# Two heads' small matmuls in turns on different rows or columns of TensorE's array, and one attention chain for two

## The chip, the cores and the metric

The kernel runs on one core of one Trainium2 chip. The metric is the device time of one execution in microseconds (us). The engines are TensorE (PE in the profile, its weight loads PEld), VectorE (DVE), ScalarE (ACT), GpSimd (POOL) and SyncE (SP). Each engine runs its own instructions in the order in which they stand in its queue; engines wait for each other by semaphores.

## The reference

Three layers on 256 tokens of width 1024, in float32. The first block is run twice: a mixer (gated delta rule and a dilated attention of 8 heads of 64) and a convolutional GLU. The second block has a mixer of three parts (gated linear attention of 4 heads with 32 key and 64 value channels, a causal convolution of width 31, a differential attention of 4 heads with two 64-wide maps each) and then a mixture of 16 experts. What the change touches, cut to its core:

```python
# first block, attention of 8 heads (three dilations, merged by their softmax denominators)
s = einsum('bqhd,bkhd->bhqk', q, k);  o = softmax(s + window) @ v
# second block, differential attention: two maps a head
a = softmax(q1 @ k1.T) - lam * softmax(q2 @ k2.T);  o = a @ v
# second block, gated linear attention, chunked in the reference
S_t = diag(alpha_t) S_{t-1} + k_t v_t^T;  o_t = q_t S_t
# which is  o = (q k^T, entry i,j times the product of alpha over j+1..i) v
```

## The kernel before

The work is one program on one core. Weights are streamed from memory, each split into a high and a low part (`wh` on ScalarE, L382, and `wl` on VectorE or GpSimd, L383), and every large product is three matmuls, L404 to L406. These fill the time between small dependent steps. In each layer a `Weave` object (L198) takes several generators ("chains") and one generator of filling matmuls: a chain yields a pair, the TensorE time that it has just used and the delay before it may go on; where no chain may go on, the filler does. Afterwards a scheduler orders each engine's instructions, so that the order on an engine is not that of the text.

The PSUM memory has eight banks, `bank(0)` to `bank(7)`, each 128 partitions of 512 floats; a bank is reused when its reader is done.

In the first mixer the chains are two of the delta rule, a preparation, two attention chains `attn(0)` and `attn(1)`, and the closing of the delta rule, `delta_out`, whose gated norm is `od` (L955). Each attention chain takes one head of a pair, `probs` (L574) computes two score matmuls (L575, 128 x 128; L576, 128 x 256) on rows 0 to 63 or 64 to 127 of the array, and the masked maxima; then the softmax goes over ScalarE and VectorE (`sm`, L1005 to L1010), three transposes (L326) put it into `pT`, and `mix_values` (L597 to L600) multiplies with the values, on columns 0 to 63 or 64 to 127. Chain 0 writes its half of bank 2, chain 1 the other half and then splits the result for the output projection. Bank 6 belongs to chain 0, bank 7 to chain 1.

In the second mixer two chains `diff(0)` and `diff(1)` do the same for the differential attention, two maps a head. The chain `gla` builds the linear attention's 4 score matrices level by level. The keys' and queries' factors of eight levels (`gX`, made on GpSimd, L1321 and L1322) give for each head and each pair of levels a block of matmuls of 32 rows (L1353; L1358 and L1361 for the last two levels; 16 blocks, twelve of L1353), in bank 3 for heads 0 and 2, in bank 4 for heads 1 and 3. After each block VectorE copies the blocks' valid parts to `gsc` under a mask (L1366). Ahead of the levels stand the diagonal blocks (L1335, L1336). The convolution's 62 taps (L1247) run on VectorE at the same time.

A matmul of 32-bit floats (without the high and low split) appears as two records in the trace.

Of the kernel before, what the change touches and what calls it, by code (L numbers as in the profile page):

```python
# [17 lines left out]
P = 128  # L18
S = 256
NT = 2  # L20
# [177 lines left out]
class Weave:  # L198
    """Lays several dependent chains and one stream of filling work into one trace order."""
# [48 lines left out]
def emit(ctx, tc, A, out, stop=None, dbg=None):  # L248
# [89 lines left out]
    def rsqrt1(ss, scale, o=None):  # L338
        """1 / sqrt(sum * scale + EPS) of one value a partition, whose sum comes in two parts."""
# [78 lines left out]
    def rows_in(t, xT, a, g, gain, done):  # L418
        """The residual step of token tile t, and its new rows, transposed and split."""
# [23 lines left out]
    def row_scales(nv, done, lag):  # L443
        """What the next norm scales the rows by: per row, and the same spread over the partitions."""
# [35 lines left out]
    def residual(t, a, g):  # L480
        """x += rmsnorm(a) * g on token tile t."""
# [31 lines left out]
    def tok_first(ps, chunks, xT, done, end, mid=None, ahead=None):  # L513
        """Two groups of products of token rows; those of the first rows go ahead of the second rows' norm."""
# [124 lines left out]
    def mixer1(l, before, held, a0):  # L639
# [355 lines left out]
        def attn(lane):  # L995
            yield lambda: "qkT" in done
            yield (0, 1.0 + 1.5 * lane)
            qT, kT = env["qk"][:, 0], env["qk"][:, 1]
            for pair in range(4):
                pr = slice(64 * lane, 64 * lane + 64)  # L1000
                hs = slice((2 * pair + lane) * 64, (2 * pair + lane) * 64 + 64)
                sm, nmx = probs(bank(6 + lane), qT[pr, pair, :], kT[pr, pair, :], cst[:, C_DB:C_DB + 384])
                ls = tmp([P, 2], tag="lsum")
                for t, (c0, c1) in enumerate(QT):
                    SC.activation(sm[:, c0:c1], sm[:, c0:c1], AF.Exp, bias=nmx[:, t:t + 1], scale=0.125)  # L1005
                    V.tensor_tensor_reduce(sm[:, c0:c1], sm[:, c0:c1], cst[:, C_DC + c0:C_DC + c1], 1.0, 0.0,
                                           op0=OP.mult, op1=OP.add, accum_out=ls[:, t:t + 1])
                V.reciprocal(ls, ls)
                for t, (c0, c1) in enumerate(QT):
                    V.tensor_scalar(sm[:, c0:c1], sm[:, c0:c1], ls[:, t:t + 1], None, op0=OP.mult)  # L1010
                yield (0.65, 3.2)
                pT = transpose_probs(6 + lane, sm)
                yield (0.33, 0.6)
                yield lambda: "v" in done
                if lane == 0:
                    env["po", pair] = bank(2)
                else:
                    yield lambda pair=pair: ("po", pair) in done
                po = env["po", pair]
# [912 lines left out]
```

## Time and profile before

| | us |
|---|---|
| median of 3 runs | 1104.01 (1103.96 to 1109.92) |
| span of the profiled execution | 1100.8 |
| median less that span | 3.2 |
| TensorE busy in it | 1052.8 (96%) |
| VectorE busy | 904.2 (82%) |
| ScalarE busy | 634.5 (58%) |
| GpSimd busy | 209.9 (19%) |

The profiled execution's own time is its span, from the first to the last instruction; the time of a run also has what lies around it, here 3.2 us by the median. The mean granted TensorE clock over the span is 0.960 of full speed, 2.4 GHz; the lower level is 1.2 GHz, a granted clock of 0.50.

In the profile the busy times say how full an engine is. The chain that ended last follows the end of the program back from step to step to what released it, so it says on which engine the time was spent. Windows give busy times stretch by stretch.

### The profile page before, as it was taken

Reading aid. Unit: us, or ns where it says so; the run is one execution under the profiler, and the core shown is the slowest. Engines: PE = TensorE matmul, PEld = TensorE weight load, DVE = VectorE, ACT = ScalarE, POOL = GpSimd, SP = SyncE. Lnnn points to the kernel's source line nnn. Section 1 sums busy time; section 2 is a strip of 40 time slices with the busy share of each in tenths; the row PEclk is TensorE's granted clock in tenths of the full one; section 3 lists DMA queues with packets and bytes.
Section 4 is the critical chain, followed back from the end, with each engine's and each line's share of the span. In section 5 each row is a group of like instructions: output and inputs, shape, how many; then the busy total and the mean of one; then the engine's idle time right before and its main releaser. Section 6 shows DMA issues by size and latency. Waiting matters only on the chain.

```text
span 1100.8 us, 17299 instructions
## 1 busy us (share of the span) xinstructions
PE 1052.8 (96%) x6156; PEld 900.5 (82%) x6156; DVE 904.2 (82%) x2073; ACT 634.5 (58%) x1139; POOL 209.9 (19%) x175
## 2 busy tenths in 40 slices
PE   8999999999999899999899999998899997999997
PEld 7879877899999788887679999996777776887785
DVE  6797797798888879868797988888889768888886
ACT  6554455666655665535466665556554234787773
POOL 3510004100000462000140000004423415123231
PEclk9999998999999999999989999999889679999999
DMA  8642025555555453401437556555532036398892
GB/s 318 216 134 77 2 94 177 190 190 174 189 179 188 153 191 117 133 21 39 153 118 225 174 180 187 189 188 157 163 106 77 20 114 233 102 333 320 320 348 89
DMA packets 51997, 181.07 MB, mean 164 GB/s; under 512 B 6050, under 2 KB 7491, under 8 KB 51907
## 3 DMA queue, kind: packets, MB, share of 16 engines
q1 hardware_dynamic: 51186, 179.33, 48.7%
q8 instruction: 50, 0.82, 0.3%
q10 hardware_dynamic: 720, 0.59, 0.2%
q14 instruction: 41, 0.33, 0.1%
HBM read 178.86 MB, written 1.05 MB: 163 GB/s over the span
## 4 chain that ended last, share of the span: by engine, by line
PE 82%; DVE 12%; ACT 2%; issue 2%; DMA 1%; POOL 0%; SPq 0%; DVEq 0%; ACTq 0%
PE b L405 22%; PE b L404 22%; PE b L406 21%; PE b L326 4%; DVE wl L383 2%; PE b L1353 2%; PE b L884 2%; DVE x L491 2%; PE b L859 2%; PE b L918 1%; DVE cy L727 1%; PE b L576 1%; PE b L1544 1%; ACT wh L382 1%; PE b L575 1%
## 5 line engine op out<-in xcount | busy, mean ns | idle before, releaser
L382 ACT CAST wh<-wr 128x1024 fp32r<-128x1024 f32 x277 | 290.2, 1049 | 202.0 <-PE b L405 95.5
L383 DVE TENSOR_TENSOR wl<-wr,wh 128x1024 fp32r<-128x1024 f32 x225 | 287.2, 1280 | 65.5 <-ACT wh L382 62.7
L383 POOL TENSOR_TENSOR wl<-wr,wh 128x1024 fp32r<-128x1024 f32 x53 | 132.9, 2515 | 747.9 <-ACT wh L382 611.8
L404 PE MATMUL b<-xh,wh 128*128 128x256 f32 x816 | 237.9, 292 | 0.2 <-ACT tokq L1470 0.2
L406 PE MATMUL b<-xh,wl 128*128 128x256 f32 x816 | 234.3, 287 | 0.0
L405 PE MATMUL b<-xl,wh 128*128 128x256 f32 x816 | 233.8, 286 | 0.0
L404 PEld LDWEIGHTS b<-xh,wh 128*128 128x128 f32 x816 | 159.0, 195 | 4.0 <-issue 2.4
L405 PEld LDWEIGHTS b<-xl,wh 128*128 128x128 f32 x816 | 159.1, 195 | 1.7 <-issue 0.5
L406 PEld LDWEIGHTS b<-xh,wl 128*128 128x128 f32 x816 | 158.8, 195 | 0.4 <-issue 0.2
L404 PE MATMUL b<-wh,xh 128*128 128x512 f32 x256 | 107.7, 424 | 3.3 <-DVE wh L382 2.3
L404 PE MATMUL b<-wh,mh 128*128 128x512 f32 x272 | 110.4, 406 | 0.0
L405 PE MATMUL b<-wl,mh 128*128 128x512 f32 x272 | 109.4, 402 | 0.0
L406 PE MATMUL b<-wh,ml 128*128 128x512 f32 x272 | 108.5, 399 | 0.0
L405 PE MATMUL b<-wl,xh 128*128 128x512 f32 x256 | 106.8, 418 | 0.3 <-DVE wl L383 0.2
L406 PE MATMUL b<-wh,xl 128*128 128x512 f32 x256 | 105.2, 412 | 0.0
L1081 DVE SCALAR_TENSOR_TENSOR fu<-fq,par,fu 128x255 f32<-128x255 f32 (+1 forms) x144 | 69.1, 480 | 2.1
L404 PEld LDWEIGHTS b<-wh,xh 128*128 128x128 f32 x256 | 50.6, 198 | 16.6 <-issue 3.7
L406 PEld LDWEIGHTS b<-wh,ml 128*128 128x128 f32 x272 | 52.2, 192 | 11.4 <-issue 0.3
L404 PEld LDWEIGHTS b<-wh,mh 128*128 128x128 f32 x272 | 52.5, 193 | 10.7 <-ACT half L609 0.3
L405 PEld LDWEIGHTS b<-wl,xh 128*128 128x128 f32 x256 | 50.6, 198 | 12.8 <-issue 3.0
L405 PEld LDWEIGHTS b<-wl,mh 128*128 128x128 f32 x272 | 52.4, 193 | 10.2 <-issue 0.9
L406 PEld LDWEIGHTS b<-wh,xl 128*128 128x128 f32 x256 | 50.6, 198 | 11.4 <-issue 0.6
(431 smaller groups left out, 1970.2 us busy)
## 6 DMA issues: line engine op xcount, KB each, us to landing
wr<-in_win SPq DMA_DIRECT2D x78, 512.0 KB, 3.6
wr<-in_up SPq DMA_DIRECT2D x72, 512.0 KB, 3.5
wr<-in_down SPq DMA_DIRECT2D x44, 512.0 KB, 3.5
wr<-in_egu SPq DMA_DIRECT2D x44, 512.0 KB, 6.0
wr<-in_wout SPq DMA_DIRECT2D x24, 512.0 KB, 3.5
wr<-in_uptok SPq DMA_DIRECT2D x16, 512.0 KB, 4.3
mh<-in_edn SPq DMA_DIRECT2D x8, 1024.0 KB, 5.0
ml<-in_edn SPq DMA_DIRECT2D x8, 1024.0 KB, 5.1
```

What stands on the lines that cost most here:

```text
L326: T.transpose(o, i, ident[:i.shape[0], :i.shape[0]])
L382: heads[:] = [(V.tensor_copy if first else SC.copy)(h, raw).ins]
L383: eng.tensor_tensor(l, raw, h.bitcast(F32), op=OP.subtract)
L404: T.matmul(o, ah, bh, start=start, stop=False)
L405: T.matmul(o, ah, bl, start=False, stop=False)
L406: T.matmul(o, al, bh, start=False, stop=stop)
L491: V.scalar_tensor_tensor(x[:, t, ns], hs[n], r, x[:, t, ns], op0=OP.mult, op1=OP.add)
L575: T.matmul(p[:, 0:128], qT[:, 0:128], kT[:, 0:128], start=True, stop=True)
L859: T.matmul(pq[:, u * 64:(u + 1) * 64], atu[:, u, 0, :], tv[:, u, :, 0, :], start=True, stop=True)
L884: T.matmul(pq[:, 256 + u * 64:256 + (u + 1) * 64], RRu[:, u, :], pn[:, u, :], start=True, stop=True)
L1081: V.scalar_tensor_tensor(u[:, d:], p[:, :S - d], cw[:, 2 - d:3 - d], u[:, d:], op0=OP.mult, op1=OP.add)
L1353: T.matmul(p[:, j * S + t * 128:j * S + t * 128 + 128], Xl[hp, ts], Xl[hp, ts], start=True, stop=True, tile_position=(32 * h, 0))
```

## The change

`probs` loses its matmuls; a new `scores` issues the score matmuls of two heads in turns, each made to follow the other by `turn`. `mix_values` takes two heads and issues their three matmuls in turns. Each pair of chains becomes one, `attn()` and `diff()`, which handles two heads a step (for `sm` the differential attention has 4 buffers instead of 3). In the linear attention two heads' level blocks, on banks 3 and 4, are issued in turns, and their copies follow after both. Docstrings are taken out, so line numbers shift: L577 of the kernel after is `turn`, and issues all matmuls in turns.

```diff
-    def probs(p, qT, kT, bias):
-        T.matmul(p[:, 0:128], qT[:, 0:128], kT[:, 0:128], start=True, stop=True)
-        T.matmul(p[:, 128:384], qT[:, 128:256], kT[:, 0:256], start=True, stop=True)
-        sm = tmp([P, 384], tag="sm", bufs=3)
+    def turn(last, o, w, m, **kw):
+        with tc.issue_after(last) if last is not None else ExitStack():
+            return T.matmul(o, w, m, **kw).ins
+    def scores(ps, qks):
+        last = None
+        for c0, c1, q0 in ((0, 128, 0), (128, 384, 128)):
+            for p, (qT, kT) in zip(ps, qks):
+                last = turn(last, p[:, c0:c1], qT[:, q0:q0 + 128], kT[:, 0:c1 - c0], start=True, stop=True)
+    def probs(p, bias, n):
+        sm = tmp([P, 384], tag="sm", bufs=n)
...
-    def mix_values(o, pT, v):
-        T.matmul(o[:, 0:128], v[0], pT[:, 0:128], start=True, stop=True)
-        T.matmul(o[:, 128:256], v[0], pT[:, 128:256], start=True, stop=False)
-        T.matmul(o[:, 128:256], v[1], pT[:, 256:384], start=False, stop=True)
+    def mix_values(os, pTs, vs):
+        last = None
+        for c, i, p0, start, stop in ((0, 0, 0, True, True), (128, 0, 128, True, False), (128, 1, 256, False, True)):
+            for o, pT, v in zip(os, pTs, vs):
+                last = turn(last, o[:, c:c + 128], v[i], pT[:, p0:p0 + 128], start=start, stop=stop)
...
-        def attn(lane):
+        def attn():
...
+                ps = [bank(6), bank(7)]
+                scores(ps, [(qT[pr, pair, :], kT[pr, pair, :]) for pr in halves])
+                sms = []
+                for p in ps:
+                    sm, nmx = probs(p, cst[:, C_DB:C_DB + 384], 3)
...
-        wv.add(attn(0))
-        wv.add(attn(1))
+        wv.add(attn())
...
-                for h in range(H):
-                    p = bank(3 + h % 2)
-                    hp = slice(32 * h, 32 * h + 32)
+                for h0 in (0, 2):
+                    ps = [bank(3), bank(4)]
+                    hs = [(p, slice(32 * h, 32 * h + 32), (32 * h, 0)) for p, h in zip(ps, (h0, h0 + 1))]
+                    last = None
...
+                            for p, hp, at_ in hs:
+                                if lv < 6:
+                                    last = turn(last, p[:, j * S + c0:j * S + c0 + 128], Xl[hp, ts], Xl[hp, ts],
+                                             start=True, stop=True, tile_position=at_)
...
-        wv.add(diff(0))
-        wv.add(diff(1))
+        wv.add(diff())
```

On TensorE's queue at the end of the first layer's attention, values and scores of one head stood as whole blocks (`pT` and `tokv` are values, `kq` scores; L918 is the delta rule, L404 to L406 the filling stream). Before:

```order
608 L598 MATMUL b_360_1687<-pT_1695,tokv_112 64x128
609 L599 MATMUL b_360_1687<-pT_1695,tokv_112 64x128
610 L600 MATMUL b_360_1687<-pT_1695,tokv_113 64x128
611 L575 MATMUL b_379_1769<-kq_1104 128x128
612 L576 MATMUL b_379_1769<-kq_1104 128x256
613 L918 MATMUL b_387_1801<-gam_1697,at_965 128x128 x2
614 L405 MATMUL b_343_1628<-wl_1792,xh_98 128x512
```

After, from the last part of the pair's scores to the transposes (L326, from `sm`) of its first softmax; the first values (row 608) and the first scores (row 609) of the two heads stand further up:

```order
620 L577 MATMUL b_376_1758<-pT_1727,tokv_113 64x128
621 L577 MATMUL b_378_1771<-kq_1104 128x128
622 L577 MATMUL b_377_1770<-kq_1104 128x256
623 L577 MATMUL b_378_1771<-kq_1104 128x256
624 L929 MATMUL b_390_1816<-gam_1690,at_965 128x128 x2
625 L404 MATMUL b_326_1553<-wh_1809,xh_98 128x512
626 L405 MATMUL b_326_1553<-wl_1810,xh_98 128x512
627 L406 MATMUL b_326_1553<-wh_1809,xl_99 128x512
628 L404 MATMUL b_327_1554<-wh_1809,xh_98 128x512
629 L405 MATMUL b_327_1554<-wl_1810,xh_98 128x512
630 L406 MATMUL b_327_1554<-wh_1809,xl_99 128x512
631 L326 MATMUL b_404_1865<-cst,sm_1776 128x128 x3
```

Two heads' matmuls now alternate, and the last softmax has two recurrence and six filling matmuls between its scores and its transposes; before, the transposes of the last two heads stood at rows 628 and 637.

On TensorE's queue at the linear attention's levels (L1353 and L577, from `gX`), before:

```order
4418 L1353 MATMUL b_1854_9540<-gX_9404 128x128 x4
4419 L405 MATMUL b_1823_9385<-wl_9591,xh_8371 128x512
4420 L1353 MATMUL b_1857_9568<-gX_9404 128x128 x4
4421 L406 MATMUL b_1823_9385<-wh_9590,xl_8372 128x512
4422 L406 MATMUL b_1822_9384<-wh_9590,xl_8372 128x512
4423 L404 MATMUL b_1823_9385<-wh_9590,xh_8371 128x512
4424 L1353 MATMUL b_1858_9578<-gX_9404 128x128 x4
```

After:

```order
4404 L577 MATMUL b_1836_9445<-gX_9324 128x128
4405 L577 MATMUL b_1837_9446<-gX_9324 128x128
4406 L577 MATMUL b_1836_9445<-gX_9324 128x128
4407 L577 MATMUL b_1837_9446<-gX_9324 128x128
4408 L577 MATMUL b_1836_9445<-gX_9324 128x128
4409 L577 MATMUL b_1837_9446<-gX_9324 128x128
4410 L577 MATMUL b_1836_9445<-gX_9324 128x128
4411 L577 MATMUL b_1837_9446<-gX_9324 128x128
4412 L406 MATMUL b_1799_9286<-wh_9569,xl_8372 128x512
```

A head's block of four became, with the other head's, eight matmuls that alternate between the two banks; the first pair stands at rows 4384, 4385 and 4392 to 4397, with other rows between. Ahead of the first level matmul stand 17 filling matmuls fewer than before.

On TensorE's queue where the first layer's delta rule ends: the transposes of `od` of the second token tile, before:

```order
692 L404 MATMUL b_408_1885<-wh_1978,mh_100 128x512
693 L326 MATMUL b_418_1933<-cst,od_107 128x128 x4
694 L405 MATMUL b_408_1885<-wl_1979,mh_100 128x512
695 L406 MATMUL b_408_1885<-wh_1978,ml_101 128x512
696 L404 MATMUL b_407_1884<-wh_1990,mh_100 128x512
```

After:

```order
672 L405 MATMUL b_409_1888<-wl_1943,mh_100 128x512
673 L326 MATMUL b_415_1909<-cst,od_107 128x128 x4
674 L406 MATMUL b_409_1888<-wh_1942,ml_101 128x512
675 L404 MATMUL b_410_1889<-wh_1942,mh_100 128x512
676 L405 MATMUL b_410_1889<-wl_1943,mh_100 128x512
677 L406 MATMUL b_410_1889<-wh_1942,ml_101 128x512
```

Between the two tiles' transposes stand 16 filling matmuls where 28 stood, and behind the second one 60 where 44 stood. On VectorE's queue two splits (L383) less stand ahead of that `od` in layer 0 and one less in layer 1.

## Rows read from the trace of the kernel before

**Rows 1.** Busy time, share of the span and instructions of each engine, from the page.
```profile
PE 1052.8 (96%) x6156; PEld 900.5 (82%) x6156; DVE 904.2 (82%) x2073; ACT 634.5 (58%) x1139; POOL 209.9 (19%) x175
```

**Rows 2.** The chain that ended last, by engine and by line, from the page.
```profile
PE 82%; DVE 12%; ACT 2%; issue 2%; DMA 1%; POOL 0%; SPq 0%; DVEq 0%; ACTq 0%
PE b L405 22%; PE b L404 22%; PE b L406 21%; PE b L326 4%; DVE wl L383 2%; PE b L1353 2%; PE b L884 2%; DVE x L491 2%; PE b L859 2%; PE b L918 1%; DVE cy L727 1%; PE b L576 1%; PE b L1544 1%; ACT wh L382 1%; PE b L575 1%
```

**Rows 3.** Windows: stretch, PE, PEld, DVE, ACT, POOL busy, granted clock, DMA share, GB/s.
```profile
90.00:135.00 45.00, 45.00 (x358) 40.20 (x358) 33.13 (x113) 19.73 (x43) 0.00 (x0) 1.00 0.10 34
800.00:815.00 15.00, 13.78 (x63) 9.87 (x61) 12.36 (x26) 7.98 (x13) 4.26 (x2) 0.99 0.41 111
830.00:850.00 20.00, 18.95 (x115) 15.15 (x114) 19.56 (x57) 9.47 (x24) 4.20 (x4) 1.00 0.17 54
850.00:870.00 20.00, 18.64 (x84) 14.79 (x85) 16.16 (x46) 6.68 (x10) 12.27 (x30) 0.73 0.08 27
870.00:890.00 20.00, 20.00 (x67) 14.82 (x65) 12.21 (x28) 2.19 (x4) 2.36 (x1) 0.50 0.22 77
```

**Rows 4.** The chain in order of time, 108 to 120 us: start, us, what.
```profile
109.31 0.41 PE b L575 x2
109.72 0.43 PE b L576 x2
...
118.19 0.36 PE b L598 x2
118.55 0.22 PE b L599 x2
118.77 0.22 PE b L600 x2
```

**Rows 5.** Timeline of PE at the diagonal blocks: start, us, instruction, count, idle before.
```profile
848.13 0.72 PE L1335 MATMUL b<-gqT,gkT 32*128 32x128 f32 x8
848.78 0.50 PE L404 MATMUL b<-wh,xh 128*128 128x512 f32 x1
...
851.36 1.55 PE L1335 MATMUL b<-gqT,gkT 32*128 32x128 f32 x8 [1.62 <-DVE gsc L1336]
852.84 0.80 PE L1312 MATMUL b<-gmr,cy 128*128 128x512 f32 x1
```

**Rows 6.** Timeline of PE, the first layer's last scores and last softmax transposes.
```profile
148.58 0.48 PE L575 MATMUL b<-kq 64*128 64x128 f32 x2
...
156.37 0.77 PE L326 MATMUL b<-cst,sm 128*128 128x128 f32 x3 [0.94 <-DVE sm L1010]
```

**Rows 7.** Timeline of DVE and of PE at `od`, layer 0 and layer 1.
```profile
169.36 0.69 DVE L955 TENSOR_TENSOR od<-od,tokk 128x512 f32<-128x512 f32 x1
170.11 0.66 PE L326 MATMUL b<-cst,od 128*128 128x128 f32 x4
...
540.87 2.71 DVE L955 TENSOR_TENSOR od<-od,tokk 128x512 f32<-128x512 f32 x1
...
543.64 0.66 PE L326 MATMUL b<-cst,od 128*128 128x128 f32 x4 [3.35 <-DVE od L955]
```

**Rows 8.** The chain in order of time, 854 to 892 us: start, us, what.
```profile
855.34 3.02 PE b L1353 x16
...
861.54 1.53 PE b L1353 x8
...
864.42 0.23 PE b L404
...
865.35 1.08 PE b L1353 x8
...
866.87 1.08 PE b L1353 x8
...
868.85 1.60 PE b L1353 x8
...
872.02 2.00 PE b L1353 x8
...
874.75 0.43 PE b L406
```

**Rows 9.** Line L1366: its instructions, and what ended the idle time before them.
```profile
L1366 DVE COPY_PREDICATED gsc<-msk,b x24: 428/440/449, 857.4 to 891.1; 128x256 f32<-128x256 int8 x24
...
  PE b L1353: 10.0, 8
```

More of the change, by code (lines that the diff above doesn't have):

```diff
@@ L993, in attn_prep @@
             done.add("qkT")
-        def attn(lane):
+        def attn():
             yield lambda: "qkT" in done
-            yield (0, 1.0 + 1.5 * lane)
+            yield (0, 1.0)
             qT, kT = env["qk"][:, 0], env["qk"][:, 1]
+            halves = (slice(0, 64), slice(64, 128))
             for pair in range(4):
[L1000 to L1013, printed above, removed]
-                yield lambda: "v" in done
[L1015 to L1019, printed above, removed]
-                mix_values(po[pr, :256], pT, [toks[2][t][:, hs] for t in range(NT)])
-                done.add(("po", pair) if lane == 0 else ("pv", pair))
-                if lane == 1:
-                    split(mh[:, 4 + pair, :], ml[:, 4 + pair, :], po[:, :256])
-                    done.add(("m", 4 + pair))
-                yield (0.65, 1.6)
-                if lane == 0:
-                    yield lambda pair=pair: ("pv", pair) in done
-            done.add("attn_end" if lane else "attn_0")
@@ new lines, in attn @@
+                yield (0.65, 4.5)
+                pTs = [transpose_probs(6 + i, sm) for i, sm in enumerate(sms)]
+                yield (0.66, 1.0)
+                yield lambda: "v" in done
+                po = bank(2)
+                mix_values([po[pr, :256] for pr in halves], pTs,
+                           [[toks[2][t][:, (2 * pair + i) * 64:(2 * pair + i + 1) * 64] for t in range(NT)] for i in range(2)])
+                split(mh[:, 4 + pair, :], ml[:, 4 + pair, :], po[:, :256])
+                done.add(("m", 4 + pair))
@@ L1030, in mixer1 @@
+                yield (0.65, 0.6)
+            done.add("attn_end")
         wv = Weave()
@@ L1343, in gla @@
                     yield (0.45, 0.5)
-                for h in range(H):
-                    p = bank(3 + h % 2)
-                    hp = slice(32 * h, 32 * h + 32)
+                for h0 in (0, 2):
+                    ps = [bank(3), bank(4)]
+                    hs = [(p, slice(32 * h, 32 * h + 32), (32 * h, 0)) for p, h in zip(ps, (h0, h0 + 1))]
+                    last = None
                     for j in range(2):
@@ new lines, in gla @@
+                    for h, p in zip((h0, h0 + 1), ps):
+                        for j in range(2):
+                            lv = 2 * lp + j
+                            if lv < 6:
+                                V.copy_predicated(
+                                    sc[:, h], msk[:, None, M_G + 128 * lv:M_G + 128 * lv + 128].to_broadcast([P, NT, 128]),
+                                    p[:, j * S:(j + 1) * S].rearrange("p (t s) -> p t s", t=NT))
+                            elif lv == 6:
+                                V.tensor_copy(sc[0:64, h, :, 64:128], p[0:64, 0:128].rearrange("p (t s) -> p t s", t=NT))
+                            else:
+                                SC.copy(scx[:, h], p[:, S:S + 128])
@@ L1374, in gla @@
+                    yield (0.87, 0.6)
             yield lambda: "gv" in done
@@ L1456, in diff @@
                 o = env["do"]
[L1457 removed]
                 v = toks[2]
[L1459 to L1463 removed]
+                for i, pT in enumerate(pTs):
+                    hs = slice((h0 + i) * 128, (h0 + i + 1) * 128)
+                    T.matmul(o[0][:, hs], pT[:, 0:128], v[0][:, hs], start=True, stop=True)
+                    T.matmul(o[1][:, hs], pT[:, 128:256], v[0][:, hs], start=True, stop=False)
+                    T.matmul(o[1][:, hs], pT[:, 256:384], v[1][:, hs], start=False, stop=True)
+                yield (1.3, 0.2)
+            done.add("diff")
         def diff_out():
[L1466 removed]
+            yield lambda: "diff" in done
             ods = []
```

107 lines of the change are left out of this document (51 added, 56 removed).

## The prediction

> **What bounds the kernel now.** I read the busy times first: TensorE is busy for 1052.8 of 1100.8 us [rows 1], so what makes the program shorter must either take work off TensorE or raise its clock. The chain that ended last says the same: 82% of it is TensorE, 12% VectorE [rows 2]. The two lines of the change that it names, the level matmuls (L1353, 2%) and the long score matmuls (L576, 1%), are some 20 and 11 us long; no part of the change reaches the weight matmuls L404 to L406, which hold 65%.
>
> Then the stages, because these shares are means over different limits [rows 3]. In the first mixer (90 to 135 us) TensorE is busy for the whole 45 us and VectorE for 33. In the second mixer the limit moves. At 800 to 815 us VectorE has 2.6 us free. At 830 to 850 us VectorE is busy for 19.56 of 20 us. From 850 to 870 us the granted clock is 0.73, and from 870 to 890 us TensorE is busy for all 20 us at a granted clock of 0.50, the 1.2 GHz level, while VectorE is busy for only 12. Those last stretches hold the level matmuls.
>
> **The change part by part, and the cost of each.** No matmul is added or removed, and no DMA. What changes is which head's matmul stands behind which, and that two chains become one.
>
> *Score pairs.* One head's score block is 0.41 + 0.43 = 0.84 us of the chain [rows 4]. Two heads use different row halves. That rows overlap can be seen in the diagonal blocks: two heads' four records each, issued together, take 0.65 us until the next matmul starts at 848.78, while the same two one after the other take 1.48 us (851.36 to 852.84) [rows 5]. Part of these 1.48 us fell into the half clock, so the gain there is bounded by 0.5 and 0.83. So a clean pair costs about one block, and saves up to 0.84. In each first-mixer layer there are four pairs, but the order below shows that later pairs are not clean: other rows stand between the two heads, and a switch of shape on either side comes back. I take 0.6 a pair, 2.4 us a layer (bounds 0 and 3.4). In the second mixer four pairs would save 3.4; two stand where VectorE has room and two where it has none, so 1.7 counts (bounds 0 and 3.4).
>
> *Value pairs.* One head is 0.36 + 0.22 + 0.22 = 0.80 us [rows 4]. Two heads on different columns are nowhere issued in turns before, so nothing shows their overlap. Four pairs a layer bound it by 0 and 3.2 us; the nearest rows are the diagonal blocks, which do overlap, but on rows. I take 1.5 us a layer.
>
> *One attention chain in the first mixer.* Before, each head's softmax ran while the other lane's matmuls went on. Now both heads' transposes wait for two softmaxes in one VectorE queue. Between the last scores and their transposes only two recurrence matmuls and six of the filling stream stand, about 1.7 us at 0.23 us a piece. In before the last lane took from 148.58 to 156.37 us, with 0.94 us of waiting on TensorE at the end [rows 6]. So the wait is between that 0.94 us and 7.8 - 1.7 = 6.1 us. Much of the 7.8 us was VectorE's work for other chains, so I take a value nearer the lower end, 2.5 us a layer. Behind the waiting transpose stand the output projection's matmuls, which nothing else can start.
>
> *The end of that mixer.* Its close is the gated norm `od` (L955). In layer 0 `od` ended as TensorE arrived; in layer 1 VectorE took 2.71 us for it and TensorE waited 3.35 us [rows 7]. So time saved ahead of it is only a longer wait there. The order puts 12 of the filling matmuls less between the two token tiles' transposes of `od` and 16 more behind: 16 x 0.23 = 3.6 us later, against two weight splits fewer on VectorE ahead of it in layer 0 (2.4 us) and one in layer 1 (1.2 us). Where `od` decides, a layer ends 1.2 and 2.4 us later; where it doesn't, 2.4 + 1.5 - 2.5 = 1.4 us earlier. Over two layers that is +3.6 to -2.8; I take 0 (outer bounds +9 with the long softmax wait, -6 with clean pairs).
>
> *Level pairs.* The twelve level blocks take 3.02 (two heads), 1.53, 1.08, 1.08, 1.60 and six times 2.00 us in the chain, 20.3 us [rows 8]. Six pairs at the half clock would be 6 x 2.00 = 12.0, at full clock 6 x 1.08 = 6.5. So the saving is 8.3 or 13.8 us; I take 8.3. Below nothing it can't go, since no matmul is added; if turns overlap no better than the two adjacent heads at 855.34 (3.02 for two, at half clock), it is 20.3 - 18.1 = 2.2 us.
>
> *Both banks held.* Before, one bank drains while the other fills. Now both are filled and then four copies of 0.44 us [rows 9] empty them, 1.8 us instead of 0.9 before the next pair may start, five times: 4.5 us more if nothing stands between. 4 to 14 filling matmuls do stand there, which cover most of it, unless VectorE's other work is ahead of the copies. VectorE waited for the level matmuls for 10.0 us [rows 9], so it has room. I take 2 us (bounds 0 and 8).
>
> The Trainium skill, page "TensorEngine Tiling (Array Packing)", section "PSUM Bottleneck", speaks against this part: tiling speeds up TensorE but not the emptying of PSUM. The 10.0 us in which VectorE waited for the blocks say that this was not so before; by the rule a pair at full clock would last its four copies and not its matmuls.
>
> *Fill moved.* 17 filling matmuls less stand ahead of the first level block, at a place where VectorE decides, so TensorE waits there and does them later: 17 x 0.23 = 3.9 us (7.3 at half clock, 0 if the levels begin earlier).
>
> *Clock.* Other matmuls between the blocks cost 0.43 us at half clock and 0.23 at full [rows 8]. At 870 to 890 us nearly six blocks of 2.00 us leave 8 us for them, all at the half clock; at 850 to 870 us a clock of 0.73 means 10.8 us at the half level, and without the 3.02 and 1.53 us of blocks 6 are left. Of these 14 us a half, 7, comes back if the half-clock stretch goes, nothing if it stays. I take half of that, 3.5 us, because the stretch holds fewer blocks.
>
> **Sum.** First mixer 0; scores of the second -1.7; levels -8.3; banks +2; fill +3.9; clock -3.5: together -7.6 us. Against the profiled 1100.8 us that is 1093.2. The runs' median, 1104.01, lies 3.2 us above the span, so I forecast 1104 - 7.6 = 1096 us, with a range of its own from 1090 to 1102. About 1% (11 us) is what a measurement of this kernel can tell from no change.
>
> **The rivals.**
> *The clock stays up.* If paired blocks keep TensorE at the 2.4 GHz level, the levels save 13.8 and what lies between them 7, and with banks +2, moved fill +3.9 and scores -1.7 it is -16.6: 1087 us; with the first mixer's best, 6 less, 1081. For it: blocks of one head went ahead of the fall, 1.08 us each at 865.35 and 866.87, 2.00 at 872.02 [rows 8], and the stretch of blocks gets shorter. Against it: two heads' blocks at 855.34 overlapped in part and ran at the half clock. Chance 0.24.
>
> *Slower: a late softmax.* The single chain leaves TensorE with no other lane's work. If each of the four pairs, not just the last, meets the transposes before its softmaxes are done, a layer waits four times the 2.5 us, twice over: 20 us, and in the second mixer, where VectorE is full, two head pairs at 3 us: 26 us less what is left of the savings (8.3 + 1.7 + 3.5 + 2 x 3.9 - 2 - 3.9 = 15.4) gives +10.6: 1115 us. It decides once the softmax of a pair takes over 4.5 us and less than that stands between. For it: the last pair has 1.7 us. Against it: before the last pair the recurrence and the stream have rows to give. Chance 0.17.
>
> *The gain is eaten.* The columns don't overlap, each pair takes its 2.0 us and 1 us of its 1.8 us of copies stands uncovered (six times 3.0 = 18 us for 20.3), and the clock stays at half: -2.3 - 1.7 + 3.9, and +1.2 + 2.4 at the ends of the layers: +3.5, 1108 us. For it: `od` in layer 1 shows VectorE as the last to come. Against it: the 10.0 us for which VectorE waited. Then the rows overlap as the change says, the columns don't, and nothing reaches the end. Chance 0.16. By the section of the Trainium skill named above it would be so wherever the copies outlast the matmuls.
>
> **How the numbers follow.** The forecast has 0.43, the rivals 0.24, 0.17 and 0.16. Faster by over 1% (below 1093) is most of the first rival, 0.22, and a quarter of the forecast, 0.10 or so: 0.32. Slower by over 1% (above 1115) is half of the slower rival, 0.08, and the upper part of the third, where the late softmax adds to it, 0.06: 0.14. The rest, 0.54, lies within 1%. The range reaches from 1084, between the clock rival and its best, to 1112, short of the slower rival's 1115; it leaves out about 0.08 below and 0.12 above.
>
> **What would show it.** Right: score pairs at about 0.85 to 1.1 us for two heads; value pairs near 0.8; level pairs at some 2 us for sixteen records or 1.1 at full clock; the stretch from the first level block to the last, 34 us before, near 24; TensorE waiting for `sm` for 2 to 3 us once a layer. Wrong: L1353's successor in the chain still at 15 us or more (the array doesn't overlap), waits of TensorE for the copies of over 4 us (banks), waits for `sm` at every pair (the single chain), or a granted clock near 1 from 855 to 890 us (the first rival).

## The result and the profile after

| | before | after |
|---|---|---|
| median of the runs measured beside each other, us | 1105.68 (4 runs) | 1090.36 (4 runs) |
| ratio, 95% interval | | 0.9868 [0.9823, 0.9913] |
| the same, measured once more | 1106.38 (11 runs) | 1094.70 (6 runs), 0.9912 [0.9877, 0.9946] |
| span of the profiled execution, us | 1100.8 | 1085.7 |
| mean granted clock in it | 0.960 | 0.970 |

The change makes the kernel faster, by 1.3% and by 0.9% in the two measurements, 12 to 15 us. The forecast was 8 us; the time lies in the range. One run in all, of `attn_only` below, took 3438 us; it is left out of its ratio.

The page after, its busy times and its chain (the rows that answer to [rows 1, 2]):

```profile
PE 1024.4 (94%) x6156; PEld 877.0 (81%) x6156; DVE 897.1 (83%) x2073; ACT 633.7 (58%) x1139; POOL 209.2 (19%) x175
...
PE 79%; DVE 16%; ACT 2%; issue 2%; POOL 0%; DMA 0%; DVEq 0%; ACTq 0%; POOLq 0%
PE b L404 21%; PE b L405 21%; PE b L406 21%; PE b L326 4%; PE b L577 2%; DVE wl L383 2%; DVE yc L1254 2%; DVE x L491 2%; PE b L895 2%; PE b L870 2%; DVE cy L738 1%; PE b L929 1%; PE b L1561 1%; DVE hres L487 1%; ACT wh L382 1%
```

TensorE is busy for 28 us less with the same 6156 matmuls (in part because fewer of them ran at the half clock), but only 15 us reach the end, and VectorE's part of the chain rises from 12% to 16%.

Two heads do overlap on the array. Lines of the timeline of TensorE after: a score pair, the waits for `sm` and the last values and scores of layer 0, then (second mixer) level pairs:

```profile
108.09 0.93 PE L577 MATMUL b<-kq 64*128 64x128 f32 x8
108.94 0.39 PE L404 MATMUL b<-xh,wh 128*128 128x256 f32 x1
...
146.52 0.33 PE L326 MATMUL b<-cst,sm 128*128 128x128 f32 x1 [1.38 <-DVE sm L1024]
...
147.91 0.87 PE L577 MATMUL b<-pT,tokv 128*64 128x128 f32 x10
148.71 0.92 PE L577 MATMUL b<-kq 64*128 64x128 f32 x6
...
153.06 0.77 PE L326 MATMUL b<-cst,sm 128*128 128x128 f32 x3 [1.39 <-DVE sm L1024]
...
850.67 1.10 PE L577 MATMUL b<-gX 32*128 32x128 f32 x12 [1.01 <-POOL gX L1329]
...
853.30 1.23 PE L577 MATMUL b<-gX 32*128 32x128 f32 x16
...
857.09 1.46 PE L577 MATMUL b<-gX 32*128 32x128 f32 x16 [0.97 <-DVE gsc L1378]
...
863.14 0.79 PE L577 MATMUL b<-gX 32*128 32x128 f32 x2
...
867.58 2.07 PE L577 MATMUL b<-gX 32*128 32x128 f32 x14
...
874.09 1.15 PE L577 MATMUL b<-gX 32*128 32x128 f32 x14
...
877.53 1.15 PE L577 MATMUL b<-gX 32*128 32x128 f32 x14
```

From 108.09 to 108.94 eight score records of two heads take 0.85 us, what four of one head took [rows 4]. Ten of a pair's twelve value records take 0.80 us (147.91 to 148.71), where six took 0.80: columns overlap as rows do. Sixteen level records take 1.15 us, or 2.0 at half clock (867.58, fourteen of them), as eight did [rows 8].

What TensorE waits for after (us in total, times, longest):

```profile
PE b L326 <- DVE sm L1024: 5.3, 3, 2.5
PE b L326 <- DVE sm L1465: 4.9, 3, 3.3
...
PE b L577 <- DVE gsc L1346: 2.1, 1, 2.1
PE b L326 <- DVE od L966: 2.1, 1, 2.1
...
PE b L577 <- DVE gsc L1378: 1.3, 2, 1.0
```

L1024 is the softmax of the first mixer, L1465 that of the second, L1346 and L1378 the diagonal's and the levels' copies out of the two banks.

What the change does is best seen in the second mixer, cut at seven events: the last transposes of `x` before it, the first and the last score, the first and the last level matmul, the first transposes of `go` (the linear attention's result), the first of `x` after it. Windows of before, with columns as in [rows 3]:

```profile
765.71:809.72 44.01, 40.10 (x205) 34.15 (x203) 36.78 (x98) 27.76 (x44) 17.86 (x10) 0.92 0.47 153
809.72:832.56 22.84, 21.41 (x110) 16.13 (x109) 21.62 (x69) 11.23 (x33) 4.78 (x2) 0.85 0.34 98
832.56:855.27 22.71, 20.29 (x117) 16.16 (x115) 22.27 (x73) 9.69 (x20) 8.37 (x18) 0.93 0.19 66
855.27:899.83 44.56, 44.56 (x181) 33.79 (x180) 28.84 (x61) 10.63 (x18) 11.25 (x17) 0.65 0.14 48
899.83:912.23 12.40, 10.68 (x61) 8.66 (x60) 11.92 (x38) 5.89 (x13) 4.02 (x2) 1.00 0.38 128
912.23:919.74 7.51, 7.51 (x35) 5.86 (x36) 4.65 (x15) 4.31 (x9) 1.35 (x1) 1.00 0.69 231
```

The same of after:

```profile
758.62:801.13 42.51, 38.60 (x205) 32.78 (x203) 36.78 (x98) 27.75 (x44) 17.88 (x10) 0.96 0.49 159
801.13:828.92 27.79, 23.49 (x156) 20.16 (x155) 25.42 (x78) 11.17 (x30) 5.50 (x2) 0.88 0.26 77
828.92:847.59 18.67, 12.14 (x55) 8.74 (x51) 16.47 (x49) 7.77 (x21) 3.44 (x4) 0.73 0.25 86
847.59:885.39 37.80, 33.54 (x190) 23.88 (x191) 30.16 (x80) 10.96 (x19) 14.18 (x30) 0.82 0.21 64
885.39:893.55 8.16, 8.16 (x53) 6.78 (x51) 6.71 (x34) 5.63 (x13) 2.37 (x1) 1.00 0.27 95
893.55:905.34 11.79, 11.61 (x53) 9.31 (x53) 7.28 (x21) 6.46 (x13) 3.82 (x2) 1.00 0.73 261
```

The stage shrinks from 154.0 to 146.7 us. Each length is a sum of three: TensorE idle (length less busy time), time lost to the half clock (length times one less the granted clock, an estimate, since it takes TensorE as busy at either level alike), and the rest, TensorE's work as it would be at full clock. Before that is 9.5 + 24.1 + 120.4; after, 19.2 + 16.9 + 110.7. The work fell by 9.7 us and idle time grew by the same 9.7, so that the 7.3 us of the stage are what was lost less to the half clock. The experiments test that reading.

The stage holds only half of the 15.1 us between these two profiled executions. It starts at 758.62 instead of 765.71 us, 7.1 us earlier, and what follows it is 0.7 us shorter. By the same sum, taken in windows of some 20 us, the part ahead of it lost 15.1 us to the half clock before and 10.0 after, and its idle time and work together went from 750.6 to 748.6 us. This loss also moves where the code of that part does not: `second_only` below, with the first mixers of before, has 13.1 us there, and three profiles with the first mixers of after have 11.7 (`attn_only`), 12.4 (`first_only`) and 16.7 us (`warm_after`). So the first mixers' own part is 2 us at most in these two profiles, and the other 5 us can't be put down to the change.

### The profile page after: what moved, and what is told of

Same layout as the page of the kernel before. It is cut to its first block, busy times and chain, and to the rows that moved or that the text cites. A ratio compares the mean times of both kernels' runs of the same rounds, so it can differ in the third digit from the quotient of the medians.

```text
span 1085.7 us, 17298 instructions
## 1 busy us (share of the span) xinstructions
PE 1024.4 (94%) x6156; PEld 877.0 (81%) x6156; DVE 897.1 (83%) x2073; ACT 633.7 (58%) x1139; POOL 209.2 (19%) x175
## 4 chain that ended last, share of the span: by engine, by line
PE 79%; DVE 16%; ACT 2%; issue 2%; POOL 0%; DMA 0%; DVEq 0%; ACTq 0%; POOLq 0%
PE b L404 21%; PE b L405 21%; PE b L406 21%; PE b L326 4%; PE b L577 2%; DVE wl L383 2%; DVE yc L1254 2%; DVE x L491 2%; PE b L895 2%; PE b L870 2%; DVE cy L738 1%; PE b L929 1%; PE b L1561 1%; DVE hres L487 1%; ACT wh L382 1%
## 5 line engine op out<-in xcount | busy, mean ns | idle before, releaser
L383 DVE TENSOR_TENSOR wl<-wr,wh 128x1024 fp32r<-128x1024 f32 x225 | 287.4, 1280 | 65.7 <-ACT wh L382 63.0
L383 POOL TENSOR_TENSOR wl<-wr,wh 128x1024 fp32r<-128x1024 f32 x53 | 132.6, 2510 | 724.3 <-ACT wh L382 611.9
L404 PE MATMUL b<-xh,wh 128*128 128x256 f32 x816 | 237.4, 291 | 2.0 <-DVE cth L1207 2.0
L406 PE MATMUL b<-xh,wl 128*128 128x256 f32 x816 | 233.5, 286 | 0.0
L404 PEld LDWEIGHTS b<-xh,wh 128*128 128x128 f32 x816 | 158.3, 194 | 5.4 <-DVE cth L1207 2.2
L406 PEld LDWEIGHTS b<-xh,wl 128*128 128x128 f32 x816 | 158.2, 194 | 0.4 <-issue 0.2
L404 PE MATMUL b<-wh,xh 128*128 128x512 f32 x256 | 107.8, 424 | 2.5 <-ACT xh L358 2.5
L404 PE MATMUL b<-wh,mh 128*128 128x512 f32 x272 | 108.5, 399 | 0.6 <-ACT half L620 0.6
L405 PE MATMUL b<-wl,mh 128*128 128x512 f32 x272 | 107.1, 394 | 0.0
L406 PE MATMUL b<-wh,ml 128*128 128x512 f32 x272 | 106.5, 392 | 0.0
L406 PE MATMUL b<-wh,xl 128*128 128x512 f32 x256 | 105.0, 411 | 0.0
L404 PEld LDWEIGHTS b<-wh,xh 128*128 128x128 f32 x256 | 50.4, 197 | 15.2 <-ACT xh L358 3.9
L406 PEld LDWEIGHTS b<-wh,ml 128*128 128x128 f32 x272 | 51.1, 188 | 10.9
L404 PEld LDWEIGHTS b<-wh,mh 128*128 128x128 f32 x272 | 51.2, 188 | 10.8 <-ACT half L620 0.8
L406 PEld LDWEIGHTS b<-wh,xl 128*128 128x128 f32 x256 | 50.3, 197 | 11.5 <-DVE xl L359 0.7
```

What stands on the lines that cost most here:

```text
L383: eng.tensor_tensor(l, raw, h.bitcast(F32), op=OP.subtract)
L404: T.matmul(o, ah, bh, start=start, stop=False)
L405: T.matmul(o, ah, bl, start=False, stop=False)
L406: T.matmul(o, al, bh, start=False, stop=stop)
```

## The experiments

Ratios are against the kernel before, run beside it on the same chip. For the stage table further down each profile was cut at the same seven events.

**The levels alone, and the attention alone.** `levels_only` is before with the levels in turns (`attn(0)`, `attn(1)`, `diff(0)`, `diff(1)` stay); `attn_only` is after with the levels head by head. The edit of `attn_only` against the kernel after (that of `levels_only` against before is the same backwards):

```diff
-                for h0 in (0, 2):
-                    ps = [bank(3), bank(4)]
+                for h in range(H):
+                    p = bank(3 + h % 2)
...
```

> The kernel before, with the linear attention's level and diagonal blocks of two heads in turns alone. Theory A (two heads' blocks overlap on the array and that shortens the second mixer): sixteen-record pairs of 1.1 us at full and 2.0 us at half clock instead of 2.2 and 4.0, the stretch from the first to the last matmul from gX about 38 us instead of 44.5, and 5 to 8 us less in all (ratio 0.993 to 0.995). Theory B (the gain comes from the new order, above all of one chain for two, not from overlap): within 3 us of before.

> The changed kernel with the linear attention's blocks head by head as before. Theory A: the level blocks at 2.0 us a head and a half clock over most of 25 us come back; 5 to 8 us less than before in all, as the two parts add up to the 15 us measured. Theory B: nearly the whole gain is kept, 12 us or more less than before.

Measured: `levels_only` 0.9962 [0.9935, 0.9988], 4 us less by the ratio and 5 by the medians, the lower edge of theory A (it had said 0.993 to 0.995); its stretch from the first to the last matmul of the levels is 35.1 us. `attn_only` is slower, 1.0049 [1.0023, 1.0074]: neither theory. The two don't add up: by the medians -5 and +7 us alone, -12 to -15 together. Two things meet here. In `attn_only` the single chain for the differential attention leaves later work to a stretch that is mostly at half clock; its window of the levels:

```profile
852.71:902.61 49.90, 49.18 (x188) 35.46 (x187) 28.97 (x81) 10.68 (x20) 14.23 (x30) 0.64 0.16 51
```

In `levels_only` the levels gain 9.5 us (44.6 to 35.1), and 8.1 of them are lost again up to the first transposes of `x`:

```profile
854.73:889.79 35.06, 32.33 (x186) 23.14 (x186) 27.57 (x54) 10.62 (x17) 11.99 (x14) 0.84 0.29 90
889.79:900.17 10.38, 5.74 (x40) 4.70 (x38) 8.35 (x37) 3.95 (x9) 2.35 (x1) 0.99 0.21 56
900.17:917.79 17.62, 13.80 (x51) 10.57 (x52) 7.95 (x28) 7.46 (x16) 1.42 (x1) 0.71 0.41 151
```

and its timeline says why:

```profile
900.17 0.66 PE L326 MATMUL b<-cst,go 128*128 128x128 f32 x2 [4.64 <-DVE hr L336]
...
902.34 0.66 PE L326 MATMUL b<-cst,go 128*128 128x128 f32 x2 [1.51 <-DVE go L1400]
...
906.27 0.80 PE L404 MATMUL b<-wh,mh 128*128 128x512 f32 x1 [2.31 <-ACT mh L355]
```

The closing norm of the linear attention leaves TensorE idle for 4.64, 1.51 and 2.31 us: the filling matmuls have gone ahead of it (119 matmul records stand between the last score and the first level in `levels_only`, 117 before, 55 after). After the whole change the same place is 8.16 us long with TensorE busy for all of them (885.39 to 893.55 above): there the single chain had left filling work to cover the norm. In `levels_only` the window that follows the idle time has a clock of 0.71.

**Turns or only pairs.** `levels_blocks` is after with the records of one head whole before those of the other, on the same two banks:

```diff
-                    for j in range(2):
-                        lv = 2 * lp + j
...
-                            for p, hp, at_ in hs:
+                    for p, hp, at_ in hs:
+                        for j in range(2):
+                            lv = 2 * lp + j
...
```

> The changed kernel with both heads' level blocks still grouped on banks 3 and 4 and their copies behind both, but the eight records of one head whole before those of the other. Theory A (turns give the overlap): a pair lasts 1.5 us at full and 3.0 us at half clock as the two adjacent blocks did before, and the kernel is 4 to 8 us slower than the changed one. Theory B: within 3 us of the changed one, since the order around the blocks is the same.

Measured: 1.0033 [1.0005, 1.006], as slow as before, 13 to 18 us worse than with turns by the ratios; theory A, and more than it said. Its timeline, first pairs of two heads adjacent, then single heads between which the scheduler put other matmuls:

```profile
860.84 2.24 PE L577 MATMUL b<-gX 32*128 32x128 f32 x16
...
864.03 3.06 PE L577 MATMUL b<-gX 32*128 32x128 f32 x16 [0.28 <-DVE gsc L1378]
...
869.45 2.07 PE L577 MATMUL b<-gX 32*128 32x128 f32 x8
...
873.03 2.07 PE L577 MATMUL b<-gX 32*128 32x128 f32 x8
```

Sixteen records take 3.06 us at the half clock where turns take 2.0, and the granted clock of the stretch is 0.61 over 43.3 us. From 869.45 us on a head's eight records stand alone, as in the kernel before; so this run tests adjacent blocks without turns in the first pairs, and blocks apart in the other six of the twelve.

`attn_blocks` does the same to scores and values, in `scores` and `mix_values`:

```diff
-        for c0, c1, q0 in ((0, 128, 0), (128, 384, 128)):
-            for p, (qT, kT) in zip(ps, qks):
+        for p, (qT, kT) in zip(ps, qks):
+            for c0, c1, q0 in ((0, 128, 0), (128, 384, 128)):
```

> The changed kernel with its single attention chains, but scores and values of one head whole before those of the other. Theory A: a pair of scores 1.5 to 1.7 us instead of 0.86, a pair of values 1.6 instead of 1.16; of some 12 us of TensorE work that comes back a third reaches the end, 3 to 6 us slower than the changed one, the rest falls into waits for the softmax. Theory B: within 2 us of the changed one.

Measured: 0.9874 [0.9844, 0.9903], the ratio of the changed kernel; theory B by that number. The reason isn't that overlap is worth nothing. Scores overlap without turns when two heads' four records stand next to each other; the timeline:

```profile
111.19 0.93 PE L577 MATMUL b<-kq 64*128 64x128 f32 x8
...
122.24 0.93 PE L577 MATMUL b<-kq 64*128 64x128 f32 x8
```

(0.86 us each to the next matmul). Eight records a head are too many for that, as 860.84 above and 855.34 of before [rows 8] show. In layer 0, from its first score to the first transposes of `x`, this kernel takes 75.7 us and the changed one 71.6 and 73.1 in its two profiles; that it isn't slower in all lies in its second mixer, whose level stretch ran at a clock of 0.95, though its levels are those of after. A second profile of the changed kernel also has 0.95 there. So the clock of one profile can't carry a verdict by itself. The four runs of `attn_blocks` had granted clocks of 0.967 to 0.972; at their clock they lie 3 to 5 us above the line of the changed kernel that is drawn further down, the 3 to 6 us of theory A. The equal ratio came with a higher clock and doesn't show that turns in scores and values are worth nothing.

**First and second mixer apart.** `first_only` has the change in both first-block mixers, `second_only` in the second mixer alone.

Against the kernel after, `first_only` has the levels of `attn_only` and

```diff
-        wv.add(diff())
+        wv.add(diff(0))
+        wv.add(diff(1))
```

(the chains themselves as before), and `second_only`, in the same way,

```diff
-        wv.add(attn())
+        wv.add(attn(0))
+        wv.add(attn(1))
```

> The change in the two first-block mixers alone (one chain, scores and values in turns); the second mixer as before. The stage times of the two profiles say 1 us less in layer 0 and 3 us less in layer 1: in all 3 to 6 us less than before. Rival (the late softmax of the single chain eats what the turns save): 0, with waits for sm of 2 us and more a layer.

> The change in the second mixer alone (one chain for the differential attention with scores in turns, levels in turns); the first mixers as before. If the stages are independent, 7 to 11 us less than before. Rival: what the levels save is given back at the end of the stage (VectorE), 3 us or less.

Measured: `first_only` 0.999 [0.996, 1.002], nothing, with 5.3 us of waits for `sm` in the two layers as in the changed kernel; the rival of its expectation. `second_only` 0.9888 [0.9814, 0.9962]: the whole gain, 12 us (4 runs; 4 to 20 us by the interval).

**Work or clock.** `levels_double` issues the matmuls of six levels twice, still in turns, so that TensorE's work in the levels is again that of head by head:

```diff
-                            for p, hp, at_ in hs:
+                            for p, hp, at_ in hs * (2 if lv < 6 else 1):
```

> The changed kernel with every L577 matmul of six of the eight levels issued twice, still in turns of two heads, so that a pair's 32 records take TensorE about as long as two heads one after the other (2.2 us at full clock, 4.0 at half); results are the same. Theory A1 (what counts is TensorE's time in the levels): as slow as the kernel with whole blocks, 14 to 18 us above the changed one. Theory A2 (the array's clock counts, and the turns keep it up, while VectorE sets the length of the stage): granted clock in the level stretch above 0.75 and at most 8 us above the changed one.

Measured: 0.9984 [0.9948, 1.0021], 8 to 13 us above the changed kernel by the ratios, with a granted clock of 0.74 in the level stretch: between the two theories. Against `levels_blocks` it has the same work at full clock (114.8 and 114.2 us) and loses less to the half clock:

| stage of the second mixer, us | length | idle | lost to half clock | work at full clock | clock of the level stretch |
|---|---|---|---|---|---|
| *levels head by head* | | | | | |
| before | 154.0 | 9.5 | 24.1 | 120.4 | 0.65 |
| first_only (this stage as before) | 159.7 | 9.5 | 30.7 | 119.5 | 0.57 |
| attn_only | 162.7 | 16.0 | 30.6 | 116.0 | 0.64 |
| levels_blocks | 161.1 | 18.0 | 28.9 | 114.2 | 0.61 |
| *levels in turns* | | | | | |
| levels_only | 153.1 | 19.5 | 18.8 | 114.8 | 0.84 |
| levels_double | 156.2 | 19.2 | 22.3 | 114.8 | 0.74 |
| after, first profile | 146.7 | 19.2 | 16.9 | 110.7 | 0.82 |
| after, second profile | 143.5 | 19.5 | 11.8 | 112.2 | 0.95 |
| second_only | 144.6 | 17.4 | 17.0 | 110.2 | 0.82 |
| attn_blocks | 143.1 | 18.9 | 12.0 | 112.3 | 0.95 |

Idle time and work together stay between 127.6 and 134.3 us in all of them, while the loss runs from 12 to 31 us. Two kernels with the same code in this stage (before and `first_only`) differ by 5.7 us, nearly all of it in that column. But the clock of the level stretch parts the two kinds without exception: 0.57 to 0.65 head by head, 0.74 to 0.95 in turns, with doubled matmuls too. The four further runs below keep to it (`taps16_before` 0.66; `taps16_after` 0.72, `warm_after` and `second_warm` 0.90).

Every run's result also has a mean granted clock, and the runs of one kernel spread along it. Some of them:

| granted clock | before, us | after, us |
|---|---|---|
| 0.954 | 1106.29 | |
| 0.958 to 0.959 | 1105.87 | 1098.70, 1098.06 |
| 0.964 | 1097.06 | 1094.63, 1094.78 |
| 0.967 | 1096.89 | 1090.51 |
| 0.970 to 0.973 | 1093.52 | 1087.47, 1086.70 |

A straight line through all 65 runs of before that have a clock on record falls by 8.4 us for each 0.01 of clock, with 1.4 us of scatter, and one through the 10 runs of the changed kernel by 8.4 too. At the same clock of 0.962 they stand at 1100.7 and 1095.3: 5.4 us are the change at a given clock. The medians of the clock are 0.957 and 0.964, and 0.007 times 840 us is 5.9: the other half. The line also sets the other kernels side by side, each at the clock of its own runs:

| kernel (runs) | mean granted clock | us above (+) or below the line of before |
|---|---|---|
| levels_only (10) | 0.963 | +1.9 |
| attn_only (6) | 0.953 | +3.3 |
| levels_blocks (10) | 0.955 | +1.0 |
| levels_double (10) | 0.963 | +1.5 |
| first_only (10) | 0.959 | -0.6 |
| second_only (4) | 0.967 | -5.1 |
| attn_blocks (4) | 0.970 | -1.2 |

So what `levels_only` gains is all in the clock, and the turns in the levels alone bring nothing at a given one; only with the second mixer's single chain, its scores in turns, do 5 us come on top (`second_only`). `levels_blocks` and `levels_double`, alike in work and alike against the line, differ by some 0.009 in the clock, 7 us: that is what the turns bring through the clock. At a given clock `levels_double` is also 7 us above the changed kernel, which is what the work itself is worth there. What exactly raises the clock stays open.

**Idle TensorE filled.** `warm_after` puts 12 full-size matmuls behind the diagonal pairs, where TensorE waits:

```diff
+                for _ in range(5 if h0 == 0 else 7):
+                    last = turn(last, ps[0][:, 256:512], ident, cst[:, 0:256], start=True, stop=True)
```

> The changed kernel with 5 and 7 extra full-size matmuls (128 x 256, results unused) behind the two diagonal pairs, where TensorE waits 2.1 us for gsc and 3.3 us for sm. Theory A2 (idle TensorE there leads to the half clock after it): granted clock of the stretch from the last score to the first level above 0.85 instead of 0.73, and 2 to 6 us less than the changed one. Rival: the waits set the time, the clock is not moved by them: within 2 us, or slower by up to 5 us if the extra matmuls are in the way.

Measured: 0.9872 [0.9806, 0.9937], 1087.59 us; not told apart from the changed kernel. The stretch ahead of the levels has a clock of 0.90 instead of 0.73, as theory A2 said, and nothing is lost by the extra work; the 2 to 6 us that it promised are not shown. The last two runs put the pieces together, with the changed kernel beside it:

> The changed kernel once more, as the ground for the next run: 1087 to 1093 us, granted clock of the level stretch between 0.8 and 0.95.

> The change in the second mixer alone, with the 12 extra full-size matmuls behind the diagonal pairs. If the first mixer's part is worth nothing and the extra matmuls keep the clock up, 2 to 5 us less than the changed kernel of the same call, and the stretch from the last score to the first level at a clock above 0.85. Rival (the clock moves by chance from run to run, whatever stands there): within 2 us.

Measured: the changed kernel 0.9912 [0.9877, 0.9946], 1094.70 us, above the 1087 to 1093 that I had written; `second_warm` 0.9832 [0.9802, 0.9862], 1086.72 us. The intervals don't meet: it is 8 us faster than the changed kernel beside it, and the fastest of the kernels that leave nothing out. Its windows, from the last score to the last level matmul:

```profile
839.20:854.92 15.72, 13.94 (x81) 10.57 (x77) 15.57 (x46) 7.53 (x21) 3.38 (x4) 1.00 0.24 81
854.92:889.29 34.37, 30.18 (x188) 21.58 (x189) 30.60 (x82) 10.82 (x19) 14.72 (x30) 0.90 0.23 74
```

The first of them is at full clock, where after has 0.73, and 3 us shorter although TensorE does more in it. All of the 8 us lie in the clock, 0.974 in the mean of its runs and 0.964 in those of the changed kernel; at a given clock it is not ahead. That the extra matmuls raise it is likely and not shown: the interval of `second_only`, the same kernel without them, overlaps, and so does that of the first measurement of the changed kernel. What speaks for them is the stretch from the last score to the first level in all fourteen profiles: where TensorE idles there for 1.8 to 3.0 us (seven of them, both with extra matmuls among these), its granted clock is 0.90 to 1.00, and where it idles for 5.4 to 6.8 us (the other seven), 0.72 to 0.80. Whether leaving out the first mixers' part adds to that was not measured by itself; `first_only` says it is worth nothing.

**Is it VectorE?** VectorE is busy for 123 to 126 us of the stage's 147 to 154, so it could set its length. `taps16_after` and `taps16_before` leave out 15 of the 31 taps of the convolution (30 operations of VectorE, 16 us in the changed kernel; the stage's busy time of VectorE falls by 9.9 us there and by 14.6 in the kernel before):

```diff
-            for j in range(1, 31):
+            for j in range(1, 16):
```

> The changed kernel with 16 of the 31 taps of the causal convolution (30 VectorE operations of about 0.5 us left out, some 15 us of VectorE's 123 in the second mixer). If VectorE sets the length of that stage at full clock, 9 to 15 us less than the changed kernel. Rival (TensorE sets it): 4 us less or nothing.

> The kernel before with the same 30 VectorE operations left out. If the half clock makes TensorE the one that ends last in the level stretch before the change, the kernel before gains less than the changed one from it: 3 to 8 us. If VectorE sets both, 9 to 15 us here too.

Measured: `taps16_after` 0.985 [0.9781, 0.992], 1084.85 us, not told apart from the changed kernel; `taps16_before` 0.9985 [0.9954, 1.0017]. By the ratios the missing operations bring nothing before and 2 to 7 us after. (By the medians it is 4.6 us before, 1105.10 to 1100.52, but at a median clock of 0.963 instead of 0.958; at a given clock the run lies 0.8 us above the line.) So VectorE's share of busy time isn't the bound. What TensorE waits for are single results that come through VectorE, as the list of waits above has them: softmax to transposes, copies to the next pair, norm to transposes. With fewer operations ahead of them they do get shorter (in `taps16_after` the stage has 13.9 us of idle time instead of 19.2), but the stage is 143.6 us long, where the changed kernel's two profiles have 146.7 and 143.5. That the waits set its length is read from the profiles and not shown by a run.

## Why the prediction was right, and where it was off

The mixers came out as the steps had it, in sign and place: nothing in the first ones, the whole gain in the second. The sum was short by 4 to 7 us. Without its clock term it was -7.6 + 3.5 = -4.1 us, and the change at a given clock measured -5.4; the clock term was -3.5, and all runs together say -5.9. So both parts were short, the clock by more.

That the sum came near is in part luck. In the second mixer scores and levels were to take 10.0 us off TensorE's work (9.7 measured), banks and fill to add 5.9 us of waiting (9.7 measured), the clock to give 3.5 (7.2 in the first profile): two errors of nearly 4 us that cancel. And the first measurement, 1.3% faster, is the outcome that had been given 0.32 against 0.54 for a change within 1%; it lies between the forecast's 1096 us and the 1087 of the rival in which the clock stays up, nearer to the rival. The second, 0.9%, is the outcome held most likely. One sign was missed: the stretch from the first of the twelve level blocks to the last, to come down from 34 to 24 us, still takes 31.0 us (847.59 to 878.61) and 27.6 in the second profile.

*Score pairs.* A clean pair takes 0.85 us, as taken. In the first mixer only the first pair is clean; the later ones come in pieces (0.42, 0.63 and 0.63 us for the second), so that a layer saves about 1.5 us, less than the 2.4 taken. In the second mixer all four pairs are clean, 0.86 to 0.95 us for two heads and 1.5 for one that met a lower clock: the eight score blocks took TensorE 7.7 us there and the four pairs 4.1, 3.6 saved where 1.7 was taken. The two times of the diagonal blocks that the step compares, 0.65 and 1.48 us [rows 5], come from the same code, one head written whole after the other; the second fell in part into the half clock, so their difference says little of what turns bring.

*Value pairs.* 0.36 + 0.80 = 1.16 us for two heads instead of 1.60: 1.8 us a layer, where 1.5 was taken. The columns do overlap, against what the third rival assumed.

*One chain in the first mixer.* Waits for `sm` are 5.3 us, 2.8 in layer 0 and 2.5 in layer 1, where 2.5 a layer was taken. In layer 0 half of it is at the last pair, as said (1.39 us at 153.06), and half at the one before (1.38 us at 146.52).

*End of the first mixer.* Layer 0 took 71.7 us before and 71.6 and 73.1 after, layer 1 75.6 and 72.4. In layer 1 `od` still comes last (wait of 2.1 us, 3.35 before [rows 7]). 0 was taken, and `first_only` measured 0.

*Level pairs.* The same twelve blocks took 20.3 us and take 9.7 now (the ten groups, each to the next matmul): 10.6 saved, 8.3 taken.

*Both banks held.* 2.1 us at the second diagonal pair and 1.3 at the levels, 3.4 against 2. What the Trainium skill says under "PSUM Bottleneck" on its page "TensorEngine Tiling (Array Packing)", that tiling speeds up TensorE but not the emptying of PSUM, doesn't decide here: with four copies of 0.43 us behind a pair of 1.1, TensorE waited for the levels' copies for only 1.3 us.

*Fill moved, the step that was wrong.* It was put down as +3.9 us of work done later. TensorE does idle more ahead of the levels: 10.8 us from the first score to the first level, 3.9 before. But the work that was moved stands where the closing norm would leave TensorE idle, and covers it: `levels_only`, which keeps the old place of the fill, idles for 8.5 us there, and its idle time in the stage is 19.5 us, 19.2 after the change. The term was right as a move and wrong as a cost; what the sum lacked in its place is that time saved in the levels meets the norm behind them, where without the moved fill 8.1 of 9.5 us are lost again.

*Clock.* -3.5 was taken for the second mixer; the first profile after says -7.2 (24.1 to 16.9), the second -12.3 (to 11.8), all runs of the kernel together -5.9. Both profiled executions are the quickest of their measurement (1087.47 and 1086.70 us), so the last is the best value. The step halved what might come back "because the stretch holds fewer blocks"; the stretch in turns had a clock of 0.82 and 0.95.

*Not in the sum:* waits of 4.9 us for the softmax of the second mixer (L1465), for which the slower rival had taken 6. That rival's other half, waits at every pair of the first mixer, did not come: 2.8 and 2.5 us a layer, not 10. `attn_only`, slower than before, shows its mechanism in part: it waits 7.9 us for the two softmaxes, before 0.9; but its second mixer also loses 6.5 us more to the half clock.

*The rivals.* "The clock stays up" came half true (0.82 and 0.95 in two profiles instead of 0.65). "Slower" holds for a part of the change alone. "The gain is eaten" holds for the first mixers.

## What to carry to other kernels

Count what a saving on the busiest engine does in three columns, its idle time, its work at full clock and what the lower clock costs: here, in the second mixer, 10 us of saved matmul time became 10 us of waiting, and of the gain over all runs about half lay in the clock. Compare two kernels at the same granted clock as well, since the runs of each follow it. Two small matmuls on different rows or columns of the array are worth putting next to each other, and in turns where a block is long (here eight records); but the filling work that is freed is worth as much as the cover it gives to the next dependent step, so see which norm or softmax comes after it. Test the parts of such a change together as well as apart, since here -5 and +7 us alone made -12 to -15.

## What was not expected of the hardware

Two heads' blocks of four records each overlap without turns when they are adjacent (0.86 us for both), blocks of eight only in part (3.0 us at half clock where turns take 2.0). Runs of one and the same kernel spread over up to 17.5 us, and nearly all of the spread goes with the mean granted clock, 8.4 us for each 0.01 of it. In fourteen profiles the level stretch had a granted clock of 0.57 to 0.66 wherever the blocks went head by head, with TensorE busy nearly throughout, and of 0.72 to 0.95 wherever they went in turns, also when their matmuls were issued twice. Twelve extra full-size matmuls in a stretch where TensorE had waited cost nothing and came with a granted clock of 0.90 and 1.00 there instead of 0.73.
